# Loads of the state-space mixer's tables between the first MLP's weights, tables begun half a chunk later, and three MLP tiles multiplied at once behind the norm

## The chip, the cores and the metric

The kernel runs on one core of a Trainium2 chip. The metric is the device time of one execution in microseconds (us); the times given are medians of several runs. A core has TensorE (PE: matrix products; PEld are its weight loads), VectorE (DVE), ScalarE (ACT), GpSimd (POOL) and SyncE (SP). SP computes nothing in this kernel; it issues DMAs, and nearly all of them.

## The reference

Two blocks stand one behind the other. In the first, each of two layers is a mixer and an MLP, with a modulation (shift, scale, gate) worked out from a conditioning vector by `ada_w`:

```python
def squared_relu_mlp(h, w1, w2):
    return jnp.square(jax.nn.relu(h @ w1)) @ w2
...
    for l in range(DEPTH):
        mod_l = (jax.nn.silu(c) @ ada_w[l] + ada_b[l]).reshape(b, ADA_CHUNKS, 1, D_MODEL)
        ...
        h_l = modulate(rmsnorm(x, norm1_g[l]), mod_l[:, 0], mod_l[:, 1])
        if l % 2 == 0:
            o_c, o_l = mla_retention_mixer(...)
        else:
            o_c, o_l = s5_mixer(...)
        x = x + mod_l[:, 2] * o_l
        h_l = modulate(rmsnorm(x, norm2_g[l]), mod_l[:, 3], mod_l[:, 4])
        x = x + mod_l[:, 5] * squared_relu_mlp(h_l, mlp_w1[l], mlp_w2[l])
        if need_ctx:
            ...
            xc = xc + mod_c[5] * squared_relu_mlp(h_c, mlp_w1[l], mlp_w2[l])
```

Layer 0 mixes by attention and retention, layer 1 by `s5_mixer`, a scan over the tokens with a state of 64 complex numbers in each of 64 groups of 16 features. What the scan needs of its parameters (the discretized matrices, their powers, a short convolution) depends on no token. D_MODEL is 1024, D_FF 4096, and layer 0's MLP works on 512 tokens (256 and 256 of context). The second block (attention over 256 tokens and another MLP) is not touched by the change.

## The kernel before

**Products in three parts.** Float32 products are made of rounded high and low parts: for each weight tile PE multiplies high by high, high by low and low by high (`mm3`). A weight unit is 128x1024 float32, 512 KB. SP loads it into one of 4 `raw` buffers (`_dma`, L356, the DMA at L360), ACT rounds it to `whi` (L375) and DVE subtracts to get `wlo` (L377), 4 buffers each. `unit` walks one list of all units in order of use; loads run LOOK_DMA = 6 units ahead of use in the program, casts LOOK_PREP = 2 units.

**Layer 0's MLP** (`mlp` with l = 0) starts with the norm: DVE writes `hmt` (L679, 16 tiles), ACT the high parts of `hm` (L681), DVE their low parts (L685). Then come 8 chunks, c0 to c7. A chunk has 4 `m1` units (24 matmuls of 128x512 each, then Relu, Square, and a split into `hidh`, cast by ACT, and `hidl`, subtracted by DVE at L723) and 4 `m2` units (24 matmuls each): 8 slots and 192 matmuls. In c0 the first two m1 tiles are multiplied together (`fmulg`): for each of 8 row blocks both tiles' products with the high part of `hm`, and last the products with its low part.

**What lies between the slots.** In chunks 0 to 5, at the slots in ADA_SLOTS, PE multiplies a pair of `ada1` units, the next layer's modulation; these are used as they land, without a cast (`raw,sc` in the rows). In every slot one step of the generator `fill` (`s5_tables`) is taken: 41 steps compute layer 1's tables (DVE products at L1397, PE transposes at L1507, copies; 16 half tables, each written to DRAM by SP as `s5wd`, `s5ld`, `s5cd`). Below, a "table" is one of these 16. When all are written, further steps load back what the scan needs first: four `s5w` and three `s5R` (L1633, L1638, 512 KB each, SP) and 16 `s5km` pieces of 128 KB (L1661, issued by POOL). 32 more `s5km` pieces of 64 KB are loaded at the start of layer 1 into `whi` and `wlo` buffers, when PE has released these.

**What sets the order.** The program is traced by a scheduler that simulates the engines and writes each engine's instructions in one order; an engine runs its own list strictly in order, and a DMA waits in its queue for its buffer and its source. `after(earlier, later)` adds a dependency that only orders two instructions and makes nobody wait on the chip.

Of the kernel before, what the change touches and what calls it, by code (L numbers as in the profile page):

```python
# [28 lines left out]
LOOK_PREP = 2  # L29
# [13 lines left out]
FIN_AT = (14, 15, 16, 17)  # L43
FIN_LATE = 4
FIN_CUT = (672, 1024, 1), (0, 672, 0)
ADA_SLOTS = (0, 2, 4, 6)
SWAP = [(a + 16) % 32 for a in range(32)]
ROT = np.concatenate([np.arange(0, 16), np.arange(32, 48), np.arange(16, 32), np.arange(48, 64)])

# [198 lines left out]
def unit_order():  # L248

    u = []  # L250

    def add(n, a, b=None):
        u.extend((n, i) for i in (range(a) if b is None else range(a, b)))

    add("wrv", 1)
    add("win", 2)
    add("wrv", 1, 4)
    add("win", 2, 12)
    add("wuq", 2)
    add("wukv", 1)  # L260
    add("win", 12, 16)
    add("ada0", 32)
    add("wout", 8)
    na = 0
    for c in range(8):
        for j in range(8):
            if j in ADA_SLOTS and c < 6:
                add("ada1", na, na + 2)
                na += 2
            i = 4 * c + j % 4  # L270
            add("m1_0" if j < 4 else "m2_0", i, i + 1)
    add("wglu", 16)
    add("m1_1", 32)
    add("m2_1", 32)
    for l in range(2):
        add(f"f1gu_{l}", 44)
        add(f"f1d_{l}", 22)
        add(f"ni_{l}", 4)
        add(f"nu_{l}", 2)
        add(f"ni_{l}", 4, 8)  # L280
        add(f"nt_{l}", 4)
        add(f"ni_{l}", 8, 12)
        add(f"no_{l}", 8)
        add(f"f2gu_{l}", 44)
        add(f"f2d_{l}", 22)
    return u
# [12 lines left out]
class K:  # L299
    def __init__(s, tc, A, out, voff, coff, ctx, dbg=None):  # L300
        s.tc, s.nc, s.A, s.out, s.dbg = tc, tc.nc, A, out, dbg or {}
        s.voff, s.coff = voff, coff
        e = ctx.enter_context
        s.ctx = ctx
        s.const = e(tc.tile_pool(name="const", bufs=1))
        s.wraw = e(tc.tile_pool(name="wraw", bufs=4))
        s.whi = e(tc.tile_pool(name="whi", bufs=4))
        s.wlo = e(tc.tile_pool(name="wlo", bufs=4))
        s.sm = e(tc.tile_pool(name="sm", bufs=2))
        s.pp = e(tc.tile_pool(name="pp", bufs=8, space=PSUM))  # L310
        s.res = e(tc.tile_pool(name="res", bufs=1, side="right"))
        s.order = unit_order()
        s.xr = s.lim = None
        s.n_dma = s.n_prep = s.n_use = 0
        s.raws, s.preps = {}, {}
        s.last = s.hold = None
        s.setup()


# [36 lines left out]
    def _dma(s, i):  # L356
        n, u = s.order[i]
        src = s.A[n][u]
        raw = s.wraw.tile([128, UC], F32, name="raw", tag="raw")
        s.nc.sync.dma_start(raw[:, :src.shape[-1]], src)  # L360
        s.raws[i] = raw, src.shape[-1]

    def load(s, n):
# [16 lines left out]
    def unit(s, name, u):  # L380
        i = s.n_use
        assert s.order[i] == (name, u), (s.order[i], name, u)
        s.n_use += 1
        last = len(s.order) - 1 if s.lim is None else s.lim
        while s.n_dma <= min(i + LOOK_DMA, last):
            s._dma(s.n_dma)
            s.n_dma += 1
            while s.n_prep <= min(s.n_dma - 1, i + LOOK_PREP):
                s._prep(s.n_prep)
                s.n_prep += 1  # L390
        while s.n_prep <= min(i + LOOK_PREP, last):
            s._prep(s.n_prep)
            s.n_prep += 1
        return s.preps.pop(i)
# [746 lines left out]
    def mlp(s, l, x, T, halves, fill=iter(()), st=None):  # L1141
        nc, tc = s.nc, s.tc
        m = s.mod[l]
        with ExitStack() as es:
# [14 lines left out]
            for c in range(32 // nf):  # L1159
                hid = []  # L1160
                for f in range(nf):
                    if l == 0:
                        if f in ADA_SLOTS:
                            next(ada, None)
                        next(fill, None)
                    cb = 0.0
                    if s.xr and f < RAW:
                        ps, cb = s.raw_get(f)
                        if f == RAW - 1:
                            s.exr.close()  # L1170
                    elif l == 0 and c == 0 and f < 2:
                        if f == 0:
                            first = [s.ps() for _ in range(2)]
                            s.fmulg([(z[:, :T], f"m1_{l}", i) for i, z in enumerate(first)], h)
                        ps = first[f]
                    elif l:
                        ps = s.ps([128, 2, T])
                        s.fmul(ps, f"m1_{l}", f, h)
                        ps = s.both(ps, s.sq.tile([128, T], F32, name="hb"))
                    else:  # L1180
                        ps = s.ps()
                        s.fmul(ps[:, :T], f"m1_{l}", c * nf + f, h)
                    r = s.sq.tile([128, T], F32, name="sq", tag="sq")
                    nc.scalar.activation(r[:, :T], ps[:, :T], AF.Relu, bias=cb)
                    q = s.sq.tile([128, T], F32, name="hn", tag="hn")
                    nc.scalar.activation(q[:, :T], r[:, :T], AF.Square)
                    if l:
                        ab = HL(hb.tile([128, 2, T], F32R, name="hid", tag="hid"))
                    else:
                        ab = tuple(hb.tile([128, T], F32R, name="hid" + n, tag="hid" + n) for n in "hl")  # L1190
                    hid.append(s.split(q[:, :T], ab))
# [13 lines left out]
                if l == 0:  # L1205
                    if c == 7:
                        s.oq = es.enter_context(tc.tile_pool(name="oq", bufs=1))
                    prep = s.s5_prep(x, c == 7)
                    for d in range(0, KT, 2):
                        if c == 7:  # L1210
                            for i in (d, d + 1):
                                s.s5_load_c(i % 4, i // 4)
                        if 4 + d // 2 in ADA_SLOTS:
                            next(ada, None)
                        hi, lo = s.unit("m2_0", c * 4 + d // 2)
                        next(fill, None)
                        ps = [s.ps() for _ in range(2)]
                        at = [(i, f) for i in range(2) for f in range(nf)]
                        if d == 0:

                            at.sort(key=lambda z: z[1] == nf - 1)
                        for i, f in at:
                            o = (i * 4 + f) * 128
                            s.mm3(ps[i][:, :T], (hi[:, o:o + 128], lo[:, o:o + 128]), hid[f], f == 0, f == nf - 1)
                            if f == nf - 1:
                                for c0, c1, mi in halves:
                                    nc.vector.scalar_tensor_tensor(x[:, d + i, c0:c1], in0=ps[i][:, c0:c1],  # L1227
                                                                   scalar=m[:, 5, d + i, mi:mi + 1],
                                                                   in1=x[:, d + i, c0:c1], op0=OP.mult, op1=OP.add)
                                next(prep, None)  # L1230
                    for _ in prep:
                        pass
# [150 lines left out]
    def s5_tables(s, es):  # L1383
# [171 lines left out]
        s.s5wp = s.s5f.enter_context(tc.tile_pool(name="s5wp", bufs=4, side="right"))  # L1555
        s.s5ws = {}
        s.s5rs = []
        for i in range(3):
            for f in range(2 if i < 2 else 0):
                s.s5_load(i, f)  # L1560
                yield
            s.s5_load_r(i)
            yield
        s.s5km = {}
        for f in range(2):
            yield from s.s5_km_steps(0, f, 4)

    def s5_prep(s, x, on):

# [55 lines left out]
    def s5_load(s, i, f):  # L1625

        p, tag = (s.wraw, "raw") if i // 2 % 2 else (s.s5wp, "s5w")
        w = p.tile([128, 2, 4, 128], F32, name="s5w", tag=tag)
        s.s5_half(w, s.s5w, i, f)
        s.s5ws[i, f] = w  # L1630

    def s5_half(s, w, src, i, f):
        s.nc.sync.dma_start(w.rearrange("p c g x -> p c (g x)"),  # L1633
                            src[i][:, :, 4 * f:4 * f + 4].rearrange("p c g x -> p c (g x)"))

    def s5_load_r(s, i):
        R = s.s5wp.tile([128, 2, 8, 64], F32, name="s5R", bufs=3)
        s.nc.sync.dma_start(R.rearrange("p c g n -> p (c g n)"), s.s5r[i].rearrange("p c g n -> p (c g n)"))  # L1638
        s.s5rs.append(R)

    def s5_load_c(s, i, f):
        p, tag = (s.s5wp, "s5w") if i > 3 and f == 0 else (s.s5cp, "s5c")
# [5 lines left out]
        for _ in s.s5_km_steps(i, f, 8):  # L1648
            pass

    def s5_km_steps(s, i, f, step):

        km = []
        n = 1 if i == 0 else 2
        for q in range(n):
# [2 lines left out]
            o = 32 * i + 16 * f + 8 * q  # L1658
            src = s.s5l[o:o + 16 // n].rearrange("g h x -> h g x")
            for j in range(8):  # L1660
                s.nc.gpsimd.dma_start(w[j::8].rearrange("p a b x -> p (a b) x"), src[0:16, :, 16 * j:16 * j + 128])  # L1661
                if j % step == step - 1:
                    yield
            km += [w[:, k] for k in range(4 // n)]
# [785 lines left out]
```

## Time and profile before

| | |
|---|---|
| median of 3 runs | 2185.43 us (2179.25 to 2187.47) |
| profiled execution | 2180.33 us, its span 2178.6 us |
| PE busy | 2022.9 us, 93% of the span |
| DVE busy | 1587.6 us, 73% |
| ACT busy | 1061.8 us, 49% |
| POOL busy | 41.6 us, 2% |
| mean granted TensorE clock | 0.963 of full speed |

An instruction's engine waits for its inputs; the profile names what ended each wait. Busy time on PE includes matmuls at a lower clock. Times inside the execution are counted from the span's start: layer 0's MLP runs from 345 to 809 us, c0 from 345.44 to 427.51.

### The profile page before, as it was taken

The page shows a single profiled execution, that of the slowest core. Times are in us where ns is not written, and L with a number is a line of the kernel's source. Part 1 is how long each engine was busy: PE and PEld are TensorE (multiplying, and loading weights), DVE is VectorE, ACT ScalarE, POOL GpSimd, SP SyncE. Part 2 cuts the span into 40 slices and gives each one's busy share as a digit, 9 for nine tenths or more (in the row PEclk, how much of TensorE's full clock was granted, in tenths as well). Part 3 has the DMA queues.
Part 4 walks back from the last instruction along what each step waited for, and adds up shares of the span by engine and source line. Part 5 has one row for each costly group of instructions (what it writes and reads, how often), then busy time and mean ns, then how long its engine had stood idle before and what let it go on. Part 6 is the DMA issues. An engine that isn't in the chain of part 4 may idle for free. (4 is left out here: it accounts for less than half of the span.)

```text
span 2178.6 us, 35381 instructions
## 1 busy us (share of the span) xinstructions
PE 2022.9 (93%) x13449; PEld 1643.5 (75%) x13449; DVE 1587.6 (73%) x3302; ACT 1061.8 (49%) x2018; POOL 41.6 (2%) x120
## 2 busy tenths in 40 slices
PE   6999998899997996799999999999999999999997
PEld 4775475576765875698888888778889888868886
DVE  6877767899972468776557778768778776868765
ACT  4553533233332344458545555546546654646653
POOL 0000000000001011000000000000000000000000
PEclk8999998999998997799999999899999999999999
DMA  8224435657777456346665666234664666415663
GB/s 300 107 85 137 172 116 174 200 179 219 247 219 224 135 170 218 119 156 192 187 194 177 191 195 195 97 98 158 190 194 155 195 192 208 148 35 174 198 190 115
DMA packets 130251, 373.41 MB, mean 171 GB/s; under 512 B 12896, under 2 KB 35360, under 8 KB 129568
## 3 DMA queue, kind: packets, MB, share of 16 engines
q1 hardware_dynamic: 128288, 366.94, 53.1%
q0 software_dynamic: 1792, 4.20, 0.8%
q8 instruction: 106, 1.74, 0.3%
q14 instruction: 65, 0.53, 0.1%
HBM read 345.33 MB, written 25.76 MB: 170 GB/s over the span
## 5 line engine op out<-in xcount | busy, mean ns | idle before, releaser
L377 DVE TENSOR_TENSOR wlo<-raw,whi 128x1024 fp32r<-128x1024 f32 (+1 forms) x491 | 597.0, 1217 | 350.8 <-ACT whi L375 347.9
L375 ACT CAST whi<-raw 128x1024 fp32r<-128x1024 f32 (+1 forms) x491 | 512.4, 1047 | 688.4 <-PE ps L328 351.7
L328 PE MATMUL ps<-xh,whi 128*128 128x512 f32 (+1 forms) x1408 | 465.0, 383 | 8.8 <-DVE xh L1903 6.6
L328 PE MATMUL ps<-xh,wlo 128*128 128x256 f32 x1312 | 359.6, 283 | 0.8 <-DVE wlo L377 0.8
L328 PEld LDWEIGHTS ps<-xh,whi 128*128 128x128 f32 x1408 | 255.9, 189 | 62.2 <-DVE xh L1903 7.9
L328 PEld LDWEIGHTS ps<-xh,wlo 128*128 128x128 f32 x1312 | 247.5, 189 | 7.0 <-DVE wlo L377 1.1
L328 PE MATMUL ps<-hm,whi 128*128 128x512 f32 x704 | 228.7, 396 | 0.8 <-DVE x L1227 0.8
L328 PE MATMUL ps<-hdh,whi 128*128 128x512 f32 x528 | 186.4, 397 | 0.0
L328 PEld LDWEIGHTS ps<-hm,whi 128*128 128x128 f32 x704 | 131.5, 188 | 37.7 <-issue 3.5
L328 PE MATMUL ps<-hm,wlo 128*128 128x512 f32 (+1 forms) x448 | 154.3, 344 | 0.0
L328 PE MATMUL ps<-hdh,wlo 128*128 128x256 f32 x528 | 147.9, 281 | 0.0
L328 PE MATMUL ps<-slab,whi 128*128 128x512 f32 x416 | 132.7, 398 | 0.3 <-ACT slabq L944 0.3
L328 PE MATMUL ps<-hidh,whi 128*128 128x512 f32 x256 | 102.1, 406 | 19.9 <-ACT whi L375 16.5
L328 PEld LDWEIGHTS ps<-hdh,whi 128*128 128x128 f32 x528 | 99.0, 188 | 24.2
L328 PE MATMUL ps<-xrl,whi 128*128 128x258 f32 x384 | 109.8, 288 | 0.0
L328 PE MATMUL ps<-xrh,whi 128*128 128x258 f32 x384 | 109.5, 289 | 0.0
L328 PE MATMUL ps<-xrh,wlo 128*128 128x258 f32 x384 | 109.5, 288 | 0.0
L328 PE MATMUL ps<-hidl,whi 128*128 128x512 f32 x256 | 102.0, 399 | 5.7 <-DVE hidl L723 5.7
L328 PE MATMUL ps<-hidh,wlo 128*128 128x512 f32 x256 | 101.6, 400 | 0.5 <-DVE wlo L377 0.5
L328 PEld LDWEIGHTS ps<-hdh,wlo 128*128 128x128 f32 x528 | 99.1, 188 | 0.3
L328 PEld LDWEIGHTS ps<-slab,whi 128*128 128x128 f32 x416 | 78.3, 190 | 18.5 <-issue 1.0
L328 PEld LDWEIGHTS ps<-hm,wlo 128*128 128x128 f32 x448 | 84.1, 188 | 10.3
(532 smaller groups left out, 3762.1 us busy)
## 6 DMA issues: line engine op xcount, KB each, us to landing
raw<-in_m_dram SPq DMA_DIRECT2D x128, 512.0 KB, 4.4
raw<-in_f1gu_dram SPq DMA_DIRECT2D x88, 512.0 KB, 4.2
raw<-in_f2gu_dram SPq DMA_DIRECT2D x88, 512.0 KB, 4.3
raw<-in_ada_dram SPq DMA_DIRECT2D x80, 512.0 KB, 4.4
raw<-in_f1d_dram SPq DMA_DIRECT2D x44, 512.0 KB, 4.2
raw<-in_f2d_dram SPq DMA_DIRECT2D x44, 512.0 KB, 3.8
raw<-in_ni_dram SPq DMA_DIRECT2D x24, 512.0 KB, 4.2
slab<-in_adaq_dram SPq DMA_DIRECT2D x32, 256.0 KB, 6.0
```

Source lines behind the costliest of these rows:

```text
L328: s.last = s.nc.tensor.matmul(out, lhsT, rhs, start=start, stop=stop)
L375: nc.scalar.copy(hi[:, :w], raw[:, :w])
L377: nc.vector.tensor_tensor(lo[:, :w], raw[:, :w], hi[:, :w], op=OP.subtract)
```

## The change

Four edits. (1) The table loads of `s5_tables` (`s5w`, `s5R`, and the first 16 `s5km`) are ordered behind the last weight load that the program has issued by then (`after(s.wdma, ...)`), one by one. (2) All 48 `s5km` DMAs go from POOL's queue to SP's; the first 16 yield to the MLP every second instead of every fourth. (3) In c0's four m1 slots `fill` takes no step, so that all its steps come 4 slots later; in c0 the ada pairs stand at slots 0, 4, 6, 7 instead of 0, 2, 4, 6. (4) Three instead of two m1 tiles are multiplied together behind the norm, with a cast look-ahead of 1 while they are set up.

```diff
-ADA_SLOTS = (0, 2, 4, 6)
+ADA_SLOTS = [(0, 4, 6, 7)] + 7 * [(0, 2, 4, 6)]
...
-        s.nc.sync.dma_start(raw[:, :src.shape[-1]], src)
+        s.wdma = s.nc.sync.dma_start(raw[:, :src.shape[-1]], src)
...
-            while s.n_prep <= min(s.n_dma - 1, i + LOOK_PREP):
+            while s.n_prep <= min(s.n_dma - 1, i + s.look):
...
-        while s.n_prep <= min(i + LOOK_PREP, last):
+        while s.n_prep <= min(i + s.look, last):
...
-                        if f in ADA_SLOTS:
+                        if f in ADA_SLOTS[c]:
                             next(ada, None)
-                        next(fill, None)
+                        if c:
+                            next(fill, None)
...
-                    elif l == 0 and c == 0 and f < 2:
+                    elif l == 0 and c == 0 and f < 3:
                         if f == 0:
-                            first = [s.ps() for _ in range(2)]
+                            s.look = 1
+                            first = [s.ps() for _ in range(3)]
                             s.fmulg([(z[:, :T], f"m1_{l}", i) for i, z in enumerate(first)], h)
+                            s.look = LOOK_PREP
...
         for i in range(3):
             for f in range(2 if i < 2 else 0):
-                s.s5_load(i, f)
+                s.after(s.wdma, s.s5_load(i, f))
                 yield
-            s.s5_load_r(i)
+            s.after(s.wdma, s.s5_load_r(i))
             yield
         s.s5km = {}
         for f in range(2):
-            yield from s.s5_km_steps(0, f, 4)
+            yield from s.s5_km_steps(0, f, 2, True)
...
-    def s5_km_steps(s, i, f, step):
+    def s5_km_steps(s, i, f, step, behind=False):
...
             for j in range(8):
-                s.nc.gpsimd.dma_start(w[j::8].rearrange("p a b x -> p (a b) x"), src[0:16, :, 16 * j:16 * j + 128])
+                z = s.nc.sync.dma_start(w[j::8].rearrange("p a b x -> p (a b) x"), src[0:16, :, 16 * j:16 * j + 128])
+                if behind:
+                    s.after(s.wdma, z)
```

**SP behind the last table.** SP's list where the last half table has been written to DRAM (`s5wd`, `s5ld`). `in_m_0_dram` are the MLP's weight units, `in_ada_dram` the modulation's. Before:

```order
154 L1509 DMA s5wd<-wt 256x1x512
155 L1527 DMA s5ld<-lt 128x240
156 L360 DMA raw<-in_ada_dram 128x1024
157 L1633 DMA s5w<-s5wd 128x2x512 x2
158 L360 DMA raw<-in_ada_dram 128x1024
159 L1638 DMA s5R<-s5rd 128x1024
160 L1633 DMA s5w<-s5wd 128x2x512 x2
161 L1638 DMA s5R<-s5rd 128x1024 x2
162 L360 DMA raw<-in_m_0_dram 128x1024 x2
```

Of the change:

```order
161 L361 DMA raw<-in_m_0_dram 128x1024 x2
162 L1638 DMA s5w<-s5wd 128x2x512
163 L361 DMA raw<-in_m_0_dram 128x1024 x3
164 L1638 DMA s5w<-s5wd 128x2x512
165 L361 DMA raw<-in_m_0_dram 128x1024
166 L1644 DMA s5R<-s5rd 128x1024
167 L1638 DMA s5w<-s5wd 128x2x512
168 L361 DMA raw<-in_m_0_dram 128x1024
169 L1638 DMA s5w<-s5wd 128x2x512
170 L361 DMA raw<-in_m_0_dram 128x1024
171 L1644 DMA s5R<-s5rd 128x1024
172 L361 DMA raw<-in_m_0_dram 128x1024
```

Seven table loads stood in a row with two ada units among them and none of the MLP's; now a weight unit or more stands between any two but one pair. Behind these rows the 16 `s5km` follow, two at a time, between weight units.

**PE in c0.** PE's list of the last of c0's m1 products. `hm` are the norm's outputs, `ident,wr`, `ident,wi` and `cw,bb` belong to a table, `raw,sc` to the modulation, `hidh` and `hidl` open the m2 products. Before:

```order
847 L328 MATMUL ps<-hm,wlo 128x512
848 L328 MATMUL ps<-hm,whi 128x512 x4
849 L328 MATMUL ps<-hm,wlo 128x512
850 L328 MATMUL ps<-raw,sc 32x512 x4
851 L1507 MATMUL ps<-ident,wr 128x128 x4
852 L328 MATMUL ps<-raw,sc 32x512 x4
853 L1507 MATMUL ps<-ident,wi 128x128 x4
854 L328 MATMUL ps<-cw,bb 32x128 x16
855 L328 MATMUL ps<-hm,whi 128x512 x2
```

Of the change:

```order
860 L329 MATMUL ps<-hm,wlo 128x512
861 L329 MATMUL ps<-hm,whi 128x512 x2
862 L329 MATMUL ps<-hm,wlo 128x512
863 L329 MATMUL ps<-raw,sc 32x512 x4
864 L329 MATMUL ps<-hidh,whi 128x512 x4
865 L329 MATMUL ps<-hidl,whi 128x512
```

The table and the ada units that stood ahead of the fourth m1 tile are gone from there: all 96 matmuls of c0's m1 half now stand in one row. One table instead of three is done on PE when c1 begins, and two more stand in c5.

**SP at the start of layer 1.** SP's list from the last load of the scan that needs no buffer of the MLP. Before:

```order
167 L1633 DMA s5c<-s5cd 128x2x512 x8
168 L1633 DMA s5w<-s5wd 128x2x512 x9
169 L1638 DMA s5R<-s5rd 128x1024
170 L1633 DMA s5w<-s5wd 128x2x512 x2
171 L1633 DMA s5c<-s5cd 128x2x512 x4
```

Of the change:

```order
190 L1638 DMA s5c<-s5cd 128x2x512 x8
191 L1638 DMA s5w<-s5wd 128x2x512 x3
192 L1666 DMA s5km<-s5ld 16x8x128 x32
193 L1638 DMA s5w<-s5wd 128x2x512 x6
194 L1644 DMA s5R<-s5rd 128x1024
195 L1638 DMA s5w<-s5wd 128x2x512 x2
```

The 32 `s5km` loads, which POOL issued, now stand in SP's list ahead of six `s5w` loads.

## Rows read from the trace of the kernel before

**Rows 1.** The page: span; part 1, busy time by engine; part 6, issue to landing.

```profile
span 2178.6 us, 35381 instructions
...
PE 2022.9 (93%) x13449; PEld 1643.5 (75%) x13449; DVE 1587.6 (73%) x3302; ACT 1061.8 (49%) x2018; POOL 41.6 (2%) x120
...
raw<-in_m_dram SPq DMA_DIRECT2D x128, 512.0 KB, 4.4
```

**Rows 2.** Windows: c0's m1 and m2, c2, c5, c6; columns: us, PE, PEld, DVE, ACT, POOL, PEclk, DMA share, GB/s.

```profile
345.44:383.56 38.12, 32.03 (x164) 20.71 (x161) 34.00 (x76) 16.02 (x31) 0.00 (x0) 0.87 0.69 230
383.56:427.51 43.95, 34.12 (x201) 22.82 (x199) 43.69 (x94) 10.03 (x15) 0.53 (x1) 0.88 0.58 187
...
480.62:537.72 57.10, 54.27 (x349) 40.10 (x345) 51.00 (x101) 19.91 (x35) 1.05 (x2) 1.00 0.71 222
...
653.32:720.90 67.58, 50.90 (x220) 38.61 (x221) 21.27 (x38) 17.04 (x23) 9.08 (x16) 0.87 0.79 234
720.90:764.85 43.95, 43.95 (x194) 36.06 (x192) 18.99 (x28) 15.41 (x21) 0.00 (x0) 1.00 0.31 99
```

**Rows 3.** Timeline of PE: one table; start, us, engine, operation, idle before and its end.

```profile
584.49 0.60 PE L1507 MATMUL ps<-ident,wr 128*128 128x128 f32 x4
585.46 0.69 PE L328 MATMUL ps<-cw,bb 64*32 64x128 f32 x32
```

**Rows 4.** Timeline of PE and ACT in c5, where PE waits.

```profile
676.68 1.46 PE L328 MATMUL ps<-raw,sc 128*32 128x512 f32 x8
692.99 1.04 ACT L375 CAST whi<-raw 128x1024 fp32r<-128x1024 f32 x1 [19.78 <-DMA raw<-in_m_dram]
694.09 0.79 PE L328 MATMUL ps<-hidh,whi 128*128 128x512 f32 x1 [15.95 <-ACT whi L375]
...
699.50 0.39 PE L328 MATMUL ps<-hidl,whi 128*128 128x512 f32 x1
```

**Rows 5.** Timeline of SP's queue in c5: table loads, then weights.

```profile
662.56 1.24 SPq L1633 DMA_DIRECT2D s5w<-s5wd  x2
...
664.96 2.52 SPq L1633 DMA_DIRECT2D s5w<-s5wd  x2
667.52 1.40 SPq L1638 DMA_DIRECT2D s5R<-s5rd  x2
670.28 3.51 SPq L360 DMA_DIRECT2D raw<-in_m_dram  x2
```

**Rows 6.** DMA issues from 660 to 694 us: KB each, median us to landing.

```profile
raw<-in_m_dram SPq DMA_DIRECT2D x2, 512.0 KB, 21.7
```

**Rows 7.** Timeline of SP's queue and of POOL at the start of layer 1.

```profile
805.19 0.52 SPq L1633 DMA_DIRECT2D s5w<-s5wd  x1
829.11 1.45 SPq L1633 DMA_DIRECT2D s5w<-s5wd  x2
...
809.21 9.44 POOL L1661 DMA_DIRECT2D s5km<-s5ld  x18 [127.80 <-PE ps L328]
818.71 7.28 POOL L1661 DMA_DIRECT2D s5km<-s5ld  x14
```

**Rows 8.** Timeline of PE in c0's m1 half.

```profile
364.55 1.07 PE L328 MATMUL ps<-raw,sc 128*32 128x512 f32 x8
367.67 0.75 PE L1507 MATMUL ps<-ident,wr 128*128 128x128 f32 x4 [2.06 <-DVE bb L1397]
372.45 3.19 PE L328 MATMUL ps<-raw,sc 128*32 128x512 f32 x8 [4.03 <-DMA raw<-in_ada_dram]
...
377.68 0.99 PE L328 MATMUL ps<-hm,whi 128*128 128x512 f32 x2
```

**Rows 9.** Timeline of PE in c0's m2 half, one wait.

```profile
394.53 0.51 PE L328 MATMUL ps<-hidl,whi 128*128 128x512 f32 x1 [2.79 <-DVE hidl L723]
```

**Rows 10.** Timeline of DVE behind the norm.

```profile
350.60 5.62 DVE L685 SCALAR_TENSOR_TENSOR hm<-hmt,mod,hm 128x256 fp32r<-128x256 f32 x14
...
358.07 0.34 DVE L1397 TENSOR_TENSOR h<-bt,qri 128x64 f32<-128x64 f32 x2
```

More of the change, by code (lines that the diff above doesn't have):

```diff
@@ L266, in unit_order @@
         for j in range(8):
-            if j in ADA_SLOTS and c < 6:
+            if j in ADA_SLOTS[c] and c < 6:
                 add("ada1", na, na + 2)
@@ L1170, in mlp @@
                             s.exr.close()
-                    elif l == 0 and c == 0 and f < 2:
+                    elif l == 0 and c == 0 and f < 3:
                         if f == 0:
-                            first = [s.ps() for _ in range(2)]
+                            s.look = 1
+                            first = [s.ps() for _ in range(3)]
                             s.fmulg([(z[:, :T], f"m1_{l}", i) for i, z in enumerate(first)], h)
+                            s.look = LOOK_PREP
                         ps = first[f]
@@ L1212, in mlp @@
                                 s.s5_load_c(i % 4, i // 4)
-                        if 4 + d // 2 in ADA_SLOTS:
+                        if 4 + d // 2 in ADA_SLOTS[c]:
                             next(ada, None)
@@ L1628, in s5_load @@
         w = p.tile([128, 2, 4, 128], F32, name="s5w", tag=tag)
-        s.s5_half(w, s.s5w, i, f)
         s.s5ws[i, f] = w
+        return s.s5_half(w, s.s5w, i, f)
     def s5_half(s, w, src, i, f):
-        s.nc.sync.dma_start(w.rearrange("p c g x -> p c (g x)"),
-                            src[i][:, :, 4 * f:4 * f + 4].rearrange("p c g x -> p c (g x)"))
+        return s.nc.sync.dma_start(w.rearrange("p c g x -> p c (g x)"),
+                                   src[i][:, :, 4 * f:4 * f + 4].rearrange("p c g x -> p c (g x)"))
     def s5_load_r(s, i):
         R = s.s5wp.tile([128, 2, 8, 64], F32, name="s5R", bufs=3)
-        s.nc.sync.dma_start(R.rearrange("p c g n -> p (c g n)"), s.s5r[i].rearrange("p c g n -> p (c g n)"))
         s.s5rs.append(R)
+        return s.nc.sync.dma_start(R.rearrange("p c g n -> p (c g n)"), s.s5r[i].rearrange("p c g n -> p (c g n)"))
     def s5_load_c(s, i, f):
```

## The prediction

> **What bounds the kernel now.** I read the page first: PE is busy 93% of the span and DVE 73% [rows 1], so what an edit can win is PE's idle or slow time in the stages that it touches. Then the windows, one for each stage of layer 0's MLP [rows 2]. c6 is the yardstick: no table, no ada unit, PE busy all of its 43.95 us at full clock, so 192 matmuls cost 43.95/192 = 0.229 us each. One pair of ada units takes 1.0 us on PE [rows 8], one table 586.15 - 584.49 = 1.66 us [rows 3]; I use 1.6, since an instruction's end laps over the next one's start.
>
> With these prices each window has work and loss:
>
> - c0, m1: 96 x 0.229 + 3 ada pairs + 1 table = 22.0 + 3.0 + 1.6 = 26.6 of 38.12: 11.5 lost.
> - c0, m2: 22.0 + 3.0 + 2 tables 3.2 = 28.2 of 43.95: 15.8 lost.
> - c2: 43.95 + 4.0 + 3 tables 4.8 = 52.75 of 57.10: 4.4 lost.
> - c5: 67.58, and here one wait makes most of the loss (below).
>
> So of layer 0's MLP c0 and c5 are loose and the middle is not; both loose stages run at a granted clock of 0.87 and 0.88, against 1.00 in c2 and c6 [rows 2]. What DVE does there tells why: in c2 it is busy 51.0 of 57.1 us, in c6, without tables, 19.0, so a table costs DVE (51.0 - 19.0)/3 = 10.7 us. In c0's m2 half DVE is busy 43.69 of 43.95: that half is DVE's, not PE's. In c5 DVE is busy 21.3 of 67.6; there DVE has room and PE waits for something else.
>
> The timeline of c5 says for what: PE ends its ada pair at 678.1 and starts the next matmul at 694.09, after 15.95 us of idle, released by ACT's cast of a weight, and ACT itself had waited 19.78 us for that weight's DMA [rows 4]. SP's queue shows the cause: seven table loads of 512 KB leave between 662.56 and 668.9, and only then, at 670.28, the two weight loads [rows 5]. These took 21.7 us to land where the usual figure is 4.4 [rows 1, 6]. Behind the idle time the clock is low: from 694.09 to 699.50 PE starts 13 matmuls, 0.416 us apiece instead of 0.229, 2.4 us lost [rows 4].
>
> **The change part by part.**
>
> *Table loads behind weights.* The two weights go out before the first table load, and then a weight stands between any two table loads but one pair. A weight unit feeds 24 x 0.229 = 5.5 us of PE. At c5's mean rate of 234 GB/s [rows 2] a 512 KB unit takes 2.2 us, so one weight and one table load take 4.5 us, less than PE needs for the weight; an ada pair adds 1 MB to every second slot and would bring this to 6.7 us, but four raw buffers stand ahead, and c6, where part of the loads now falls, moves only 99 GB/s. I take the stall and its low clock as gone: 15.95 + 2.4 = **-18**. Bounds: 0 (the stall only moves) and -21.0, which is c5's whole excess over its work (67.58 less 43.95, a table's 1.6 and an ada pair's 1.0).
>
> *Three m1 tiles at once, no table in c0's m1.* The order shows 96 matmuls of the norm's outputs with nothing between. Before, PE reaches the ada pair at 364.55 and the fourth tile only at 377.68 [rows 8]: of these 13.1 us two ada pairs and a table are 3.6, and the rest is waits for DVE's table product (2.06 idle), for an ada unit (4.03 idle) and half speed behind them (3.19 us for a pair worth 1.0). That is 9.5 of the 11.5 lost; the other 2 are ada pairs that break into the first tiles. After, the low parts of the norm must be there when the high products of three tiles end: 48 x 0.229 = 11 us from 345.44, so at 356.4. DVE finished the low parts at 358.07 with two weight subtractions of 1.2 us between them [rows 10]; in DVE's changed list these stand ahead of the norm, so they end near 355.7. So m1 takes about 22 us and its ada pairs and table go elsewhere at their price: **-11**. Bounds: -11.5, and -5 if the low parts or the fourth weight come some 6 us late, about what PE waited for its two late inputs (2.06 + 4.03).
>
> *c0's m2.* The tables start on DVE right behind the norm as before, so PE still meets DVE subtractions of `hidl` that stand behind table products (2.79 us of waiting at one of them) [rows 9]. But two of three tables leave c0, 2 x 10.7 = 21.4 us of DVE time. c0's two halves then hold 34.0 + 43.7 - 21.4 = 56.3 us of DVE work, where they last 82.07 now; PE has 26.6 + 28.2 - 3.2 = 51.6. So all of c0 cannot come below about 56.3: from 82.07 that is -25.8, of which 3.2 is PE work that only moves, so -22.6 for both halves and -11.6 for this one. I take two thirds of it, **-8**, since waits like [rows 9] stay; bounds 0 (PE still in DVE's hands) and -11.6.
>
> *What is given back.* Two more tables are computed in c5. The PE work, 3.2, is only moved. DVE in c5 would have 21.3 + 21.4 = 42.7 us of work in a chunk of some 55, close to c2's share, and c2 loses 4.4: **+4**, bounds 0 and +8 (twice that, if the last tables also hold up the loads behind them).
>
> *s5km on SP.* 16 pieces among the weights of c5 to c7, and 32 in a row at the start of layer 1. POOL issued 18 in 9.44 us, 0.52 each; SP's dearest pair there is 1.45, 0.72 each [rows 7]. SP issues nothing between 805.7 and 829.11, 23.4 us [rows 7], and the 32 cost 16.6 to 23.0, so they fit from 809, when PE gives the buffers free, at the low price (825.8) and reach to 832 at the high one. **0**, covered by that idle queue; if the cover were gone, +17 to +23. The Trainium skill, "DMA: Bandwidth & Descriptors", section "Issuing engines are not separate DMA queues", says that DMAs run on the same 16 engines whoever issues them, and that issuing from several saves only the sequencer's time. By that, moving them cannot speed their landing and can only cost SP's issue time, which is the slower rival below. The trace neither confirms nor denies it, since no piece is issued by SP before.
>
> The sum: -18 - 11 - 8 + 4 + 0 = **-33**, from the profiled execution's 2180.33 to 2147. The span is 1.7 shorter than that time, and the median of the runs shown, 2185.43, is 5.1 above it; a median of the changed kernel may lie up to as much above my sum. I forecast **2148**.
>
> **The rivals.**
>
> *B: the gain in c0 is given back.* If DVE is as much a bound as PE over c0 to c5, the time that c0 gains returns where the two tables now stand, and only the stall counts: 2180.3 - 18 = **2162**. For it: c0's m2 half has no idle DVE, c2 is 89% DVE. Against: c5 has 46 us without DVE work, of which 16 go with the stall, and 21 are asked for.
>
> *C: the stall only moves.* Seven loads of 512 KB and 2 MB of `s5km` still have to come while weights are read, and a table load that waits in SP's queue for the write of its source (`s5ld`, `s5wd`) now holds every weight behind it. Then c0's -19 stays, and c5 keeps its 18 but for what the +4 hid: 2180.3 - 19 = **2161**. For it: DMA share is 0.79 in c5 already, and the last table is later than before, nearer to its loads. Against: c6 has a share of 0.31 [rows 2], and two weights now go first.
>
> *D: no change*, **2180**: both gains fail, because the waits only change their names.
>
> *E: slower.* SP issues 32 `s5km` ahead of six `s5w` loads, and the scan waits for those. It decides from the point where one issue takes more than 23.4/32 = 0.73 us, and it outweighs -33 when 32 issues last 23.4 + 33, 1.8 us each; slower by 0.5% (11 us) asks for 67/32 = 2.1 us each, then **2191** or more. For it: SP's pair of `s5w` at 0.72 is near the first point, and a list of 16-row pieces is a different shape than those that SP issues now. Against: POOL's 0.52 for the same pieces, a quarter of 2.1.
>
> **How the numbers follow.** Likeliest (both stalls shrink) 0.47, with its own range of 2134 to 2158 from the bounds of its terms; B 0.22, C 0.13, D 0.11, E 0.07. A range that holds B and C and the fast bound of the likeliest (-21.0 - 11.5 - 11.6 + 0 = -44, 2136, less a little for waits not counted) leaves out E, most of D and a tail: **2131 to 2173**. Half a per cent, 11 us, is about what a measurement of this kernel tells from no change. Likeliest, B and C are faster by more than that, 0.82; D is the same, 0.11; E is slower, 0.07.
>
> **What the profile of the changed kernel would show.** The stall: no wait of PE above 3 us for a weight's cast between the last table and c6, the two weight loads ahead of the first `s5w` landing in well under 10 us, and c5 with a clock near 1.00 and some 57 us long. c0: its 96 products in about 22 us from the norm's end, and c0 as a whole near 60 instead of 82. DVE above 80% in c5. The `s5km` issues on SP 0.5 to 0.7 us each, done by about 830, and the scan beginning as long after the MLP as before. Wrong it would be if DVE's table products held up `hidl` in c1 to c5 more than now (B), if a cast still ended a long wait of PE somewhere in c5 to c7 (C), or if PE's first matmul with an `s5w` came later behind the end of the MLP than before (E).

## The result, and the profile after

| | before | after |
|---|---|---|
| median | 2182.39 us (4 runs, 2179.25 to 2187.47) | 2150.25 us (4 runs, 2146.51 to 2153.46) |
| span of the profiled execution | 2178.6 us | 2149.3 us |
| mean granted clock | 0.963 | 0.968 |

The ratio is 0.9858, 95% interval 0.9833 to 0.9883: faster by 1.4%, 32 us between the medians and 29.3 between the profiled spans. The forecast of 2148 and its range hold, and the total is within 4 us of the sum's -33. Its terms are another matter: by stages two of them are wrong by 6 and 12 us, of opposite signs.

The page after (span, busy time by engine, loads of the MLP's weights from issue to landing; before in [rows 1]):

```profile
span 2149.3 us, 35341 instructions
...
PE 2019.1 (94%) x13449; PEld 1644.2 (76%) x13449; DVE 1589.7 (74%) x3302; ACT 1062.2 (49%) x2018; POOL 16.3 (1%) x72
...
raw<-in_m_dram SPq DMA_DIRECT2D x128, 512.0 KB, 4.0
```

The work is the same; PE's 2019 us of it lie closer. The windows say where (columns as in [rows 2]): c0's m1 and m2 half, then c1, c2, c3, c4, c5 and c6.

```profile
345.26:368.44 23.18, 23.18 (x109) 18.11 (x105) 23.18 (x54) 10.78 (x22) 0.00 (x0) 1.00 0.36 124
368.44:395.73 27.29, 27.29 (x157) 19.66 (x153) 24.95 (x59) 7.50 (x13) 0.00 (x0) 1.00 0.68 211
...
395.73:456.29 60.56, 57.59 (x353) 42.95 (x349) 58.86 (x119) 20.68 (x33) 1.05 (x2) 0.94 0.69 229
456.29:522.37 66.08, 59.09 (x349) 41.45 (x345) 56.65 (x109) 19.49 (x32) 0.53 (x1) 0.95 0.63 207
522.37:583.27 60.90, 57.91 (x391) 43.40 (x389) 51.86 (x105) 20.71 (x36) 1.05 (x2) 0.97 0.71 222
583.27:640.44 57.17, 54.96 (x348) 40.20 (x344) 52.52 (x105) 19.24 (x33) 0.53 (x1) 1.00 0.76 237
640.44:692.63 52.19, 51.46 (x305) 39.36 (x301) 28.06 (x49) 20.40 (x34) 1.56 (x1) 1.00 0.77 264
...
692.63:736.57 43.94, 43.94 (x193) 36.06 (x192) 18.99 (x28) 15.40 (x21) 0.00 (x0) 1.00 0.53 157
```

Before, c1, c3 and c4, which [rows 2] leaves out:

```profile
427.51:480.62 53.11, 51.78 (x332) 40.61 (x325) 49.28 (x100) 17.34 (x31) 0.53 (x1) 1.00 0.59 172
537.72:592.79 55.07, 54.34 (x353) 40.69 (x349) 50.80 (x104) 19.87 (x33) 1.06 (x2) 1.00 0.83 259
592.79:653.32 60.53, 56.69 (x389) 41.59 (x385) 46.85 (x90) 20.53 (x36) 1.04 (x1) 1.00 0.68 212
```

The table sets the windows side by side, with "work" by the prediction's prices (0.229 us for a matmul, 1.0 for an ada pair, 1.6 for a table) and "lost" as length less work. By PE's instructions the change moves three ada pairs from c0 (6 to 3) to c1 (1 to 4), and tables from c0 (3 to 1) and c4 (4 to 3) to c3 (3 to 4) and c5 (0 to 2); c1 and c2 keep 3 tables, c2 to c4 keep 4 ada pairs and c5 keeps 3.

| stage | length before | after | difference | lost before | lost after | DVE busy before | after |
|---|---|---|---|---|---|---|---|
| c0, m1 | 38.12 | 23.18 | -14.9 | 11.5 | 0.2 | 34.0 | 23.2 |
| c0, m2 | 43.95 | 27.29 | -16.7 | 15.8 | 1.7 | 43.7 | 25.0 |
| c1 | 53.11 | 60.56 | +7.5 | 3.4 | 7.8 | 49.3 | 58.9 |
| c2 | 57.10 | 66.08 | +9.0 | 4.3 | 13.3 | 51.0 | 56.7 |
| c3 | 55.07 | 60.90 | +5.8 | 2.3 | 6.6 | 50.8 | 51.9 |
| c4 | 60.53 | 57.17 | -3.4 | 6.2 | 4.4 | 46.9 | 52.5 |
| c5 | 67.58 | 52.19 | -15.4 | 20.6 | 2.0 | 21.3 | 28.1 |
| c6 | 43.95 | 43.94 | 0 | 0 | 0 | 19.0 | 19.0 |
| c7 to the first `s5w` product | 62.32 | 63.42 | +1.1 | | | | |

From the first `s5w` product to the end the spans differ by 2.1 us (1351.4 and 1349.3). Over all kernels below that stretch lies between 1349 and 1361 us, so a whole span of one execution says little below 6 us, and the stages say more.

c0 and c5 gave 47.0 us, and c1 to c4 took 18.9 of them back. 3.0 of the 18.9 are the three ada pairs. Of the other 15.9, 6.4 are more idle time of PE, and 9.5 are PE being busy longer on the same work: behind the waits the granted clock is 0.94 to 0.97 in c1 to c3, where it was 1.00. In c5 the SP queue reads as forecast: two weights ahead of the first table load (they landed 3.6 and 4.8 us after their issue), then weights and table loads in turn.

```profile
668.51 0.52 SPq L1513 DMA_DIRECT2D s5wd<-wt  x1
669.35 0.33 SPq L1531 DMA_DIRECT2D s5ld<-lt  x1
672.48 1.79 SPq L361 DMA_DIRECT2D raw<-in_m_dram  x2
674.46 0.58 SPq L1638 DMA_DIRECT2D s5w<-s5wd  x1
678.49 2.74 SPq L361 DMA_DIRECT2D raw<-in_m_dram  x3
681.27 0.55 SPq L1638 DMA_DIRECT2D s5w<-s5wd  x1
681.92 0.54 SPq L361 DMA_DIRECT2D raw<-in_m_dram  x1
...
782.22 22.56 SPq L1666 DMA_DIRECT2D s5km<-s5ld  x32
804.88 4.59 SPq L1638 DMA_DIRECT2D s5w<-s5wd  x6
```

The last two rows are the start of layer 1: 32 `s5km` issues in 22.56 us, 0.70 each, and the six `s5w` behind them at 804.88, 4.9 us after PE's first product with an `s5w` at 799.99 (before, 1.9 us after it, 829.11 and 827.17).

The middle is new. Timelines of PE, SP and DVE at the longest wait of c2, and PE's wait in c1:

```profile
426.81 1.08 PE L1511 MATMUL ps<-ident,wi 128*128 128x128 f32 x4 [2.97 <-DVE wi L1401]
...
454.51 1.72 SPq L1531 DMA_DIRECT2D s5ld<-lt  x1
456.38 2.96 SPq L361 DMA_DIRECT2D raw<-in_m_dram  x2
463.87 1.22 DVE L378 TENSOR_TENSOR wlo<-raw,whi 128x1024 fp32r<-128x1024 f32 x1 [4.15 <-ACT whi L376]
465.12 0.80 SPq L361 DMA_DIRECT2D raw<-in_ada_dram  x2
468.76 3.18 PE L329 MATMUL ps<-raw,sc 128*32 128x512 f32 x8 [5.11 <-DMA raw<-in_ada_dram]
```

In c1 PE waits for DVE's table product. In c2 it waits for an ada unit; that left SP at 465.12, when DVE had given its buffer free at 465.09 by the subtraction of 463.87, which had waited for a weight that left SP at 456.38, behind the write of a table (`s5ld`). One may read this as DVE's pace or as SP's queue; the experiments had to tell.

### The profile page after: what moved, and what is told of

It reads as the page before. It is cut to its first block, busy times and chain, and to the rows that moved or that the text cites. A ratio compares the mean times of both kernels' runs of the same rounds, so it can differ in the third digit from the quotient of the medians.

```text
span 2149.3 us, 35341 instructions
## 1 busy us (share of the span) xinstructions
PE 2019.1 (94%) x13449; PEld 1644.2 (76%) x13449; DVE 1589.7 (74%) x3302; ACT 1062.2 (49%) x2018; POOL 16.3 (1%) x72
```

## The experiments

All ratios are against runs of the kernel before made beside the experiment; their medians lie between 2181.35 and 2184.16 us. Where a median is set against the changed kernel's 2150.25, the two come from different groups of runs, so a difference of some 3 us says little there. Theory 1: c5's stall is a matter of who stands first in shared transfers, and c0 to c4 run at DVE's pace, so that what c0 wins is spent there again. The rivals stand in each expectation.

### One part alone

**e1_ties_alone** (kernel before, `s5km` left on POOL):

```diff
-        s.nc.sync.dma_start(raw[:, :src.shape[-1]], src)
+        s.wdma = s.nc.sync.dma_start(raw[:, :src.shape[-1]], src)
...
-                s.s5_load(i, f)
+                s.after(s.wdma, s.s5_load(i, f))
...
-            s.s5_load_r(i)
+            s.after(s.wdma, s.s5_load_r(i))
...
```

> Before with only the ties of the seven s5w and s5R loads (s5km stays on POOL, untied). Theory 1 (the stall of c5 is the row of table loads ahead of the weights, and c0 to c4 run at the pace of DVE, so that the two have nothing to do with each other): PE's wait of 16 us in c5 falls below 4, c5 loses 14 to 20 us, c0 to c4 stay within 3 us in sum, and the whole is 14 to 20 us faster (2162 to 2168). Theory 2 (the stall is made as much by the 16 s5km pieces of POOL's queue, which share the transfer with the weights): the weights still take over 10 us to land and less than half of the stall goes, 0 to 8 us.

2185.44 us, ratio 1.0028 (1.0016 to 1.0040): a little slower. c0 to c4 are within 2.1 us of before in each window (36.9, 46.0, 52.5, 55.9, 55.2, 61.8). In c5 (65.0 us) the wait for the first two weights is gone, and another has come (timelines of SP, ACT and PE):

```profile
695.03 0.52 SPq L1633 DMA_DIRECT2D s5w<-s5wd  x1
695.88 0.33 SPq L360 DMA_DIRECT2D raw<-in_m_dram  x1
703.10 1.04 ACT L375 CAST whi<-raw 128x1024 fp32r<-128x1024 f32 x1 [3.78 <-DMA raw<-in_m_dram]
704.05 0.58 ACT L573 COPY adas<-ps 128x512 f32<-128x512 f32 x1
704.69 1.12 PE L576 MATMUL ps<-ident,adas 128*128 128x128 f32 x4 [9.59 <-ACT adas L573]
```

`adas` is the modulation's result, which ACT copies. PE's product for it had ended at 695.10; but the copy stands in ACT's list behind the cast of a weight, and that weight, which left SP at 695.88 behind a table load, came only at 703.0. So PE waits for a weight as before, for a later one. The expectation missed: rival C of the prediction holds for this part alone, the stall moves.

**e2_km_on_sp_alone** (kernel before):

```diff
-                s.nc.gpsimd.dma_start(w[j::8]...
+                s.nc.sync.dma_start(w[j::8]...
```

> Before with only the s5km loads moved from POOL to SP. Theory 1: the two weights stand behind seven table loads and six s5km pieces now, but the bytes ahead of them are about those that POOL's queue moved beside them, so the stall stays within 4 us of 16; at the start of layer 1 the 32 issues fit into SP's idle stretch; the whole within 5 us of before. Theory 2 (POOL's pieces were what held the weights): the stall falls by half, 8 us faster. A slower result by over 10 us would mean that SP's issue of s5km delays the scan.

2174.65 us, ratio 0.9978 (0.9964 to 0.9993): 7 us faster, theory 2's size. The stall fell from 15.95 to 8.51 [rows 4]. Timeline of PE, and DMA issues from 663 to 697 us (KB, median us to landing):

```profile
688.32 0.79 PE L328 MATMUL ps<-hidh,whi 128*128 128x512 f32 x1 [8.51 <-ACT whi L375]
...
s5km<-s5ld SPq DMA_DIRECT2D x16, 128.0 KB, 7.6
raw<-in_m_dram SPq DMA_DIRECT2D x4, 512.0 KB, 7.6
s5R<-s5rd SPq DMA_DIRECT2D x3, 512.0 KB, 10.6
```

Before, `s5R` took 22.9 us in the same stretch. While POOL's 16 pieces ran, SP's loads of 512 KB landed 2.8 to 5.7 us apart, and 1.3 apart once they had ended; with all in one queue they land 1.3 to 2.1 apart from the start, where no piece stands between two of them. But the whole took as long: before, the pieces had landed by 688.9 and the two weights by 694.25; here the weights by 689.3 and the pieces by 695.3. So the move changes who is served first, not the rate (264 and 271 GB/s over the stretch). This is what the Trainium skill says in "DMA: Bandwidth & Descriptors", section "Issuing engines are not separate DMA queues": all run on the same 16 engines, and the rate that hardly changes agrees with it. In these two traces the choice of the queue still decides which load waits.

**e3_late_alone** (kernel before):

```diff
-ADA_SLOTS = (0, 2, 4, 6)
+ADA_SLOTS = [(0, 4, 6, 7)] + 7 * [(0, 2, 4, 6)]
...
-                        next(fill, None)
+                        if c:
+                            next(fill, None)
...
```

> Before with only the tables' steps begun 4 slots later and c0's ada pairs at 0, 4, 6, 7. Theory 1: c0 gets 10 to 20 us shorter, c1 to c4 together 8 to 15 us longer, since DVE has nearly the same work before the last table; the stall of c5 stays (seven loads still stand in a row, one weight ahead): 3 to 10 us faster in all. Theory 2 (waits in c0 are local and cost nothing later): c0's gain stays, 12 us or more faster.

2162.74 us, ratio 0.9928 (0.9906 to 0.9950): 18.6 faster, theory 2's size (12 or more) and not theory 1's (3 to 10). The stages have theory 1's mechanism all the same: c0 is 53.8 us long instead of 82.1 (-28.3), c1 to c4 240.3 instead of 225.8 (+14.5). What theory 1 missed is c5: its longest wait is 8.05 instead of 15.95. It is a wait for `adas` as in e1, behind a weight that left SP at 674.19 between table loads and landed at 686.29. The last table now comes behind c5's ada units (landed by 665.72, the first table load left at 672.84), which I had not expected; that this shortens the wait is argued, not shown.

**e4_three_alone** (kernel before; c0's ada pairs at 0, 4, 6, 7, which the order of units asks for):

```diff
-                    elif l == 0 and c == 0 and f < 2:
+                    elif l == 0 and c == 0 and f < 3:
...
-                            first = [s.ps() for _ in range(2)]
+                            s.look = 1
+                            first = [s.ps() for _ in range(3)]
...
```

> Before with only the three tiles multiplied at once, the shorter look-ahead and c0's ada pairs at 0, 4, 6, 7 (the tables' steps as before). Theory 1: c0's m1 half 8 to 14 us shorter, nearly all of it given back by the end of c4, where DVE ends the last table as late as before; the stall of c5 stays: within 5 us of before. Theory 2: c0's gain stays, 8 us or more faster.

2180.56 us, ratio 0.9995 (0.9981 to 1.0008): nothing. c0's m1 half is 38.06 us (before 38.12), so there was no gain in c0 to give back: PE still waits in c0 for ada units (8.2 us in all) and for DVE's table products (3.9).

### The change without one part

**e5_no_ties**, **e6_km_on_pool**, **e7_early_tables**, **e8_two_tiles**: the changed kernel with

```diff
 e5
-                s.after(s.wdma, s.s5_load(i, f))
+                s.s5_load(i, f)
...
-            s.after(s.wdma, s.s5_load_r(i))
+            s.s5_load_r(i)
...
-            yield from s.s5_km_steps(0, f, 2, True)
+            yield from s.s5_km_steps(0, f, 2)
 e6
-                z = s.nc.sync.dma_start(w[j::8]...
-                if behind:
-                    s.after(s.wdma, z)
+                z = s.nc.gpsimd.dma_start(w[j::8]...
 e7
-                        if c:
-                            next(fill, None)
+                        next(fill, None)
 e8
-                    elif l == 0 and c == 0 and f < 3:
+                    elif l == 0 and c == 0 and f < 2:
...
-                            s.look = 1
-                            first = [s.ps() for _ in range(3)]
+                            first = [s.ps() for _ in range(2)]
```

> The changed kernel without its ties (s5w, s5R and the first s5km free of any order to the weights; s5km still on SP). Theory 1 (the stall of c5 is a queue: all loads share one transfer rate, and who is issued first lands first; the ties set who): a wait of 5 to 12 us comes back in c5 or c6, where a weight or an ada unit stands behind the row of table loads, and the kernel is 5 to 12 us slower than the changed one (2156 to 2162). Theory 2 (late tables and s5km on SP already remove the stall): within 3 us of the changed kernel's 2150.

2155.82 us, ratio 0.9880 (0.9860 to 0.9899), 5.6 above the changed kernel's median; the intervals overlap. In the profile c5 is 56.92 instead of 52.19, with a wait of 3.92 us for `adas` in it, behind a weight that left SP at 675.52, after two table loads. That is theory 1's sign; the wait is below its 5 to 12 us, and the median alone doesn't decide between the theories.

> The changed kernel with its s5km loads back on POOL's queue, not tied (s5w and s5R still tied). Theory 1: POOL's pieces take their share of the transfer rate ahead of the weights again; weights issued in that stretch take over 8 us to land, PE waits 3 to 10 us somewhere in c5 or c6, 4 to 10 us slower than the changed kernel (2154 to 2160). Theory 2 (only the issue moved, nothing is gained): within 3 us.

2151.91 us, ratio 0.9865 (0.9848 to 0.9883): the same as the changed kernel; c5 lasts 52.17 and no new wait shows. Weights issued beside POOL's pieces did take 10.8 to 17.8 us to land (677.69 to 695.48 the longest), as theory 1 has it, but PE waits for none of them. With the other parts in place POOL's pieces do no harm: theory 2, and e2's gain is not added to the others.

> The changed kernel with the tables' steps begun in c0's m1 half as before (ties, s5km on SP and three tiles stay). Theory 1 (all of c0's gain comes from the tables' late start): c0 is 78 to 83 us long again, c1 to c4 get back to about 226 us, and the table loads run beside the last ada units in c5, where PE waits some 5 us: 15 to 22 us slower than the changed kernel (2165 to 2172). Theory 2 (three tiles at once carry part of it): c0 below 72 us, 10 us slower or less.

2162.92 us, ratio 0.9918 (0.9901 to 0.9935), 12.7 above the changed kernel. Windows of c0's halves and of c5:

```profile
345.34:383.51 38.17, 30.86 (x161) 20.84 (x158) 35.25 (x85) 13.87 (x29) 0.00 (x0) 0.91 0.60 204
383.51:426.13 42.62, 34.21 (x205) 22.41 (x204) 40.76 (x84) 10.11 (x15) 0.53 (x1) 0.88 0.64 200
648.16:701.92 53.76, 49.91 (x224) 38.05 (x221) 21.26 (x37) 17.60 (x26) 0.00 (x0) 0.97 0.77 263
```

c0 is as long as before although three tiles are multiplied at once: all of its gain comes from the tables' late start. c1 to c4 are back at 222.0. c5 keeps a wait of 3.85 us for `adas`, behind a weight that left SP at 679.89, after a table load. Late tables cost 22.7 us in c1 to c4 for 30.3 in c0. The whole, 12.7 us, lies between the figures of the two theories (15 to 22, 10 or less); the stages are theory 1's.

> The changed kernel with two tiles multiplied at once instead of three (look-ahead as before). Theory 1 (three tiles are worth nothing once the tables are out of the way, or only what PE waits for the norm's low parts): c0's m1 half 0 to 3 us longer and the whole within 3 us of the changed kernel. Theory 2 (the third tile hides the norm's low parts): c0's m1 half 5 us or more longer and the whole 3 us or more slower.

2150.23 us, ratio 0.9855 (0.9838 to 0.9871): the changed kernel's time. c0's halves are 24.35 and 29.42 instead of 23.18 and 27.29, and c1 to c4 240.4 instead of 244.7: the third tile wins 3.3 us in c0, and the whole shows none of it. That c1 to c4 give them back is not shown, since kernels with the same vector work differ by more than that there (below).

### What holds c1 to c4

**e9_less_dve**, **e10_writes_on_pool**, **e11_tables_a_chunk_later**, all from the changed kernel, and **e12_later_rot_on_pool** from e11:

```diff
 e9
...
-                tt(t1, lo(c), hi(0), OP.mult)
-                tt(t2, lo(1 - c), hi(1), OP.mult)
-                tt(R[:, c].rearrange("p g (b a) -> p g b a", a=8), t1, t2, op)
+                tt(R[:, c].rearrange("p g (b a) -> p g b a", a=8), lo(c), hi(0), OP.mult)
...
 e10 (so too for s5wd, s5ld, s5cd, bt and ct)
-            nc.sync.dma_start(s.s5r[u]...
+            G.dma_start(s.s5r[u]...
 e11 (in the m2 loop)
-                        next(fill, None)
+                        if c:
+                            next(fill, None)
...
-            yield from s.s5_km_steps(0, f, 2, True)
+            yield from s.s5_km_steps(0, f, 4, True)
 e12
...
-                tt(t1, lo(c), hi(0), OP.mult)
-                tt(t2, lo(1 - c), hi(1), OP.mult)
-                tt(R[:, c].rearrange("p g (b a) -> p g b a", a=8), t1, t2, op)
+                q2 = tp2.tile(sh, F32, name="q2")
+                r = R[:, c].rearrange("p g (b a) -> p g b a", a=8)
+                G.tensor_tensor(r, lo(c), hi(0), op=OP.mult)
+                G.tensor_tensor(q2, lo(1 - c), hi(1), op=OP.mult)
+                G.tensor_tensor(r, r, q2, op=op)
```

> The changed kernel with two thirds of the rotation tables' products left out (2 instead of 6 vector operations of 128x512 for each of 8 u, so those tables are not the reference's): 32 operations of 0.68 us, 22 us of DVE work less between c0 and c5, nothing else. Theory 1 (c1 to c4 run at DVE's pace, which is why they take 245 us where PE's work is 213): they get 10 us or more shorter and the kernel 8 to 18 us faster than the changed one. Theory 3 (they wait for weights and ada units that stand behind the tables' writes in SP's queue, and DVE only looks busy): 5 us faster or less.

2138.25 us, ratio 0.9791 (0.9774 to 0.9807): 12 us below the changed kernel for 22 us of DVE work. Windows of c1 to c3:

```profile
395.34:450.37 55.03, 54.30 (x353) 40.57 (x349) 51.44 (x102) 20.15 (x33) 1.05 (x2) 1.00 0.79 262
450.37:504.17 53.80, 53.80 (x349) 40.36 (x345) 51.91 (x106) 19.19 (x32) 0.53 (x1) 1.00 0.84 263
504.17:561.16 56.99, 56.26 (x393) 42.16 (x389) 53.61 (x107) 20.60 (x35) 1.06 (x2) 1.00 0.80 249
```

165.8 us instead of 187.5; the waits for the ada unit in c2 and for the table in c1 are gone, though SP's list still has the writes ahead of the weights, and the clock is at full. That speaks for theory 1; but with less vector work the tables' writes come sooner too, so theory 3 needs the next run. c4 is 3.4 us longer; c1 to c5 together 18.3 shorter, all of it in c1 to c4, where DVE's busy time fell by 15.1 (219.9 to 204.8). The whole gained less, 12, since the stretch from the first `s5w` product on was 1355.9 in this execution (1349.3 in the changed kernel's).

> The changed kernel with the tables' small traffic (bt and ct in, s5wd, s5ld, s5cd and s5rd out) issued by POOL instead of SP, so that no weight or ada load stands behind a write that waits for a table. Theory 1 (DVE's pace): the waits for ada loads in c2 go, but others come: within 4 us of the changed kernel. Theory 3 (SP's queue): the wait of 5 us in c2 and that of 3 us in c3 go and are not replaced, 5 to 12 us faster. Slower than the changed kernel if POOL's queue takes its share of the transfers at a worse moment.

2151.13 us, ratio 0.9852 (0.9830 to 0.9874): the changed kernel's time. Timeline of PE, the longest waits in c1 and c2:

```profile
429.75 1.09 PE L1511 MATMUL ps<-ident,wi 128*128 128x128 f32 x4 [6.21 <-DVE bb L1401]
...
468.95 3.00 PE L329 MATMUL ps<-raw,sc 128*32 128x512 f32 x8 [3.29 <-DMA raw<-in_ada_dram]
```

The wait for the ada unit shrinks from 5.11 to 3.29, and the wait for DVE's table in c1 grows from 2.97 to 6.21. Theory 3's 5 to 12 us don't come: the queue was mostly the place where DVE's lateness showed. c1 to c4 last 239.6, at the short end of the 240.3 to 248.3 of the kernels with late tables and the writes on SP; a share of a few us for the queue is not excluded.

> The changed kernel with the tables begun at c1 instead of in c0's m2 half, s5km again 4 to a step so that the steps fit in the slots. Theory 1 (what counts is how much table work is moved to c5, which has room): c5 holds four tables, c0 loses its last wait, c1 to c4 lose one to two tables' share, 2 to 8 us faster. Theory 3 (c1 to c3 lose by their own queue, the same wherever the tables begin): within 3 us, or slower where the last tables end so late that their loads meet c7 and the start of layer 1.

2143.52 us, ratio 0.9815 (0.9797 to 0.9834): 6.7 us below the changed kernel, the fastest of those that do all of the work. Windows of c1, c2 and c5:

```profile
393.01:448.20 55.19, 54.46 (x353) 40.81 (x349) 48.96 (x93) 19.54 (x31) 0.53 (x1) 1.00 0.66 211
448.20:506.54 58.34, 55.25 (x348) 40.40 (x344) 52.89 (x107) 19.29 (x33) 0.53 (x1) 1.00 0.77 240
616.12:680.52 64.40, 57.11 (x384) 42.94 (x380) 48.39 (x95) 22.30 (x37) 1.97 (x1) 0.95 0.72 221
```

c1 to c4 last 223.1 instead of 244.7 and c5, with four tables, 64.4 instead of 52.2: DVE's 48.4 us have gone where it had room. c5 pays for two more tables (3.2 by price) and with a wait of 5.96 us for `adas`, which was 0.73 in the changed kernel.

> The kernel whose tables begin at c1, with the rotation tables' 48 products (32 us of DVE work) given to POOL, which computes nothing in that stretch. Theory 1 (DVE's work between c0 and the last table sets the time of c1 to c4): c1 to c4 get 3 to 10 us shorter than in the kernel without it (223 us there, 211 is PE's own work), and the whole reaches 2134 to 2141. Theory 4 (POOL's products hold up DVE's, because both read and write the same memory, or POOL ends them so late that the last table waits): DVE's products of 128x512 get longer than 0.68 us, and the kernel is no faster than 2143, or slower.

2165.96 us, ratio 0.9918 (0.9894 to 0.9942): 22 us slower than e11, theory 4. Windows of c1 and c2, and DVE's timeline in c1:

```profile
392.31:457.50 65.19, 57.13 (x352) 42.21 (x348) 60.14 (x85) 19.64 (x31) 39.01 (x26) 0.95 0.59 192
457.50:532.59 75.09, 62.39 (x349) 44.49 (x345) 67.08 (x98) 19.46 (x33) 36.88 (x25) 0.86 0.66 207
...
425.60 3.23 DVE L1402 TENSOR_TENSOR t<-pi,bb 128x512 f32<-128x512 f32 x2
428.75 3.35 DVE L1402 TENSOR_TENSOR g<-ct,pc 128x576 f32<-128x576 f32 x2
432.03 1.55 DVE L724 TENSOR_TENSOR hidl<-hn,hidh 128x512 fp32r<-128x512 f32 x1
```

Two DVE products take 3.23 us beside POOL's where the changed kernel's take 1.28, and a `hidl` 1.55 instead of 0.68; DVE is busier than in e11 (60.1 and 67.1 us instead of 49.0 and 52.9) although the rotations' products have left it. Where POOL's products have ended the slowness ends too: c3, with POOL busy for 1.05 us, lasts 55.1 (e11 55.6). The Trainium skill, "SBUF — State Buffer", section "SBUF: two separate sides", states that DVE and GpSimd share one port pair, held for a whole instruction, and that a DVE operation with two inputs in SBUF takes part in this when the GpSimd operation reads SBUF: the trace agrees, these are such operations.

**All kernels together.** The time of c1 to c4 goes with DVE's busy time in them: 222.0 to 228.5 us where DVE is busy for 197 to 199 (before, e1, e2, e4, e7), 223.1 at 200.2 (e11), 226.4 at 204.8 (e9), 239.6 to 248.3 at 217 to 220 (changed, e3, e5, e6, e8, e10); e12, whose vector products are longer, stands apart with 251.9 at 216.2. So what the late tables cost there stands out in every pair of kernels, but kernels with the same vector work differ by up to 8.7 us, and its size in one execution is known to some 4 us.

## Why the prediction held, step by step

The total held in part by luck: one term was 6 us too small and one was 12 us off the other way. By stages the losses changed by -11.3 - 14.1 + 15.9 - 18.6 = -28.1, where the sum has -33.

- **The stall, -18: right in c5, wrong in its cause.** c5's loss fell from 20.6 to 2.0, -18.6. (The bound of -21.0 took a table and one ada pair as c5's work; it held no table and three pairs, so its loss was 20.6.) But the step gave it all to the weights ahead of the table loads; by e1 these ties alone only move the wait to a later weight (9.59 us). Three parts shorten it: late tables alone leave 8.05 (e3), `s5km` on SP alone 8.51 (e2), and of the kernels with two of the three, ties and late tables leave 0.7 (e6), as much as the whole change, the others 3.9 (e5, e7). In the changed kernel c5's last ada pair leaves SP from 660.08 to 661.6, ahead of the first table load at 674.46; before, it left at 677.77, behind all seven table loads. Which loads ahead of the late weight make its wait is not taken apart further.
- **Three tiles and no table in c0's m1, -11: right in size (-11.3 lost), wrong in the name.** Three tiles give nothing by themselves (e4) and nothing in the whole (e8); the table and the ada pairs out of the way give it (e3), and with the early tables back it is gone (e7). The late start without the new ada slots was not run.
- **c0's m2, -8: too small.** Its loss fell by 14.1. DVE's work in c0 fell by 29.6 us (77.7 to 48.1), not by the 21.4 of two tables, so that its bound of 56.3 for c0 did not hold (50.5 measured). The bound also took only the tables' 3.2 us of PE work as moved; three ada pairs, 3.0 us, left c0 too.
- **What is given back, +4 in c5: the step that failed.** Counting tables in PE's list, I had two leave c0 and two arrive in c5, with nothing changed between. On DVE every table begins four slots later, and c1 to c4 got 22.0 us more DVE work (197.9 to 219.9), c5 only 6.8. c1 to c4 lost 32.1 us instead of 16.2: +15.9 where the sum has 0, and c5 paid nothing for its share. That is rival B's mechanism, at 15.9 of 25.4 and in other chunks than B had it; e9 and e11 show that it is DVE's work that does it, e10 that SP's queue is not the cause of most of it. The sign that the prediction named for B did not show it: PE's waits for `hidl` in c1 to c4 are 2.5 us in all, before 2.9; the time went into waits for an ada unit (5.1), `adas` (3.0) and a table product (3.0), and into the lower clock behind them.
- **`s5km` on SP, 0: right.** 0.70 us each, at the upper end of 0.52 to 0.72; c7 up to the first `s5w` product is 1.1 us longer, 63.4, and 62.1 with `s5km` on POOL (e6); but e3 and e4, with `s5km` on POOL, have 63.5 and e7, with it on SP, 62.4, so a delay as in rival E is not shown. Wrong was that the move can only cost SP's time: alone it gains 7 us in the median (e2), and beside the other parts nothing (e6).

What c5 would look like was right (clock 1.00, 52 us for a forecast of 57), DVE above 80% in c5 was wrong (28.1 of 52.2), c0 "near 60" came to 50.5. The slow end of the likeliest case's own range, 2158, is not the sum of its slow bounds (0, -5, 0 and +8, which give 2183). Left open: why e1 is slower than before by 4 us (in its profile c0 to c6 are 2.2 us shorter, and the stretch from the first `s5w` product to the end is 1358.2 instead of 1351.4), and what makes the stretch behind layer 0 differ by up to 12 us between kernels.

## What to carry to other kernels

Where two engines are both near 90%, as PE and DVE in c1 to c4, moving work in time need not remove its cost: look for a stage in which the second engine really has room, and count its work there by its own list and windows, not by the first engine's list. In this kernel a wait for a transfer moved to the next load that was needed unless what stood ahead of it went later; test each part alone and the whole without each part, since gains for one stall don't add. An idle engine is no free helper when its operations make the busy engine's longer, as POOL's did here.

## What was not expected of the hardware

- DMAs from POOL's and SP's queues at once (before) moved data at about the rate of SP's queue alone (e2), 264 GB/s against 271, but SP's 512 KB loads then landed 2.8 to 5.7 us apart instead of 1.3 to 2.1.
- In e12 POOL's float32 products of 128x512 took 1.4 to 1.7 us in the mean, and DVE's beside them up to 1.6 instead of 0.68.
